# A hybrid attention block on one core: a third of the stick-breaking products on GpSimd, and low parts of the up weight issued after a gate addition

## The chip, the cores and the metric

One Trainium2 chip, one core of it. The metric is the device time of one launch in microseconds, the median of three runs. TensorE is called PE here, VectorE DVE, ScalarE ACT, GpSimd POOL, and SP is the engine whose queue issues nearly all DMAs.

## The reference

One layer over 2048 tokens of width 1024, in float32:

```python
u   = rms_norm(x, norm1_w)
dq, dk, dv, sq, sk, sv = split(u @ w_in)
y_diff = diff_attention(...)           # 4 heads, two softmax maps each
# stick-breaking, 8 heads of 64, strictly causal (s < t):
z = sq @ sk.T * 64 ** -0.5
log_1mb = where(mask, log_sigmoid(-z), 0.0)
rem = cumsum(log_1mb, reverse=True) - log_1mb
a = where(mask, exp(log_sigmoid(z) + rem), 0.0)
y_sb = rms_norm(a @ sv)
h = x + concat(y_diff, y_sb) @ w_out
u2 = rms_norm(h, norm2_w)
out = h + (silu(u2 @ w_gate) * (u2 @ w_up)) @ w_down      # hidden width 2816
```

## The kernel before

Every float32 operand is split into two float16 parts, a high one and a low one, so that a float32 product is three float16 products on PE. The Tile framework orders each engine's instructions: it takes the program's order, priorities and its own estimate of times, and writes one fixed queue per engine. An engine runs its queue in order and waits at each instruction for what it needs.

**Attention, first half of the program.** Eight groups `g` run one after another, four of differential attention (one head each) and four of stick-breaking attention (two heads each). While a group's attention runs, the projection of the next group is fed in between (`proj`, lines 325 to 335); behind the last group the output projection runs (L766). In a stick-breaking group, `stage_a(i, m, b)` handles 128 queries (tile `i`), one head `m` and one block `b` of up to 1024 keys. It goes through the block from the last key to the first in chunks of up to 512 (`c`). Per chunk PE writes the scores into a PSUM bank `sc` (L453), ACT takes sigmoid(-z) into the SBUF tile `om` (L559) and sigmoid(z) in place in the bank (L560), DVE runs a product scan over `om` (L562, which carries from chunk to chunk; its second operand `sc` is bypassed), and DVE multiplies sigmoid(z) with the shifted `om` into the SBUF tile `be` (L563). Tiles `om` and `be` both come from a ring of nine and are called z in the profile. Then `split_t` casts the block's `be` to float16 on ACT (`s`, L89), subtracts on POOL for the low part (L98), and one DMA transposes both (`aT`, L408). `stage_b` multiplies them with the values on PE (`yp`, L463), up to five blocks later (`PD`).

Which engine takes an operation that has a choice is decided by `pick`: it adds the estimated cost to a running load per engine and takes the lowest. `note` adds the loads of operations without a choice, and `level` sets all to zero every four query tiles.

**Feed-forward, second half.** Two token halves of 1024, each in 11 steps of 256 hidden columns (`fg`). A step computes the gate product, then (if two steps have gathered) the down product, and then the up product. In token half 0 the even steps from the third on (i = 2, 4, ..., 10) hold a down product, the odd ones don't. Gate and up are Strassen-Winograd schemes of seven products (`quad`): twelve matmuls of 128 x 512 each (L943), in the order of the code below, into PSUM banks `pa`, `pm` and `pd`. DVE makes the sums: u2 (L956), u3 (L960), c22 (L966, reads `pd`), then L974 and L977. The last product accumulates into the same bank `pd`. In half 0 the weights are prepared on the fly (`load_ffn`): SP loads a float32 buffer `fst`, ACT makes the high parts (L215), POOL forms the Winograd sums (`sx`, and in place in `fst`, L98), and DVE makes the low parts (`split_weight`, L220). A weight has four such pairs: blocks 0-1, 2-3, 4-5 and 6. Blocks 4-5 come out of the in-place sums and are the last in the queues. The up weight of step i is prepared at the end of step i - 1. In half 1 the prepared weights are read back from HBM.

Of the kernel before, what the change touches and what calls it, by code (L numbers as in the profile page):

```python
# [59 lines left out]
def block(tc, a, out):  # L60
# [3 lines left out]
    with top:  # L64
# [8 lines left out]
        def note(e, ns):  # L73
            load[e] += ns * KW[e]
# [34 lines left out]
        def nm(s):  # L109
            uid[0] += 1  # L110
            return f"{s}{uid[0]}"
# [92 lines left out]
            scale_end(lambda m: across(m, pt, cols), rW, pW, junk is not None, sW)  # L204
            return sW

        casts = []

        def behind(k):
            return tc.issue_after(casts[min(k, len(casts) - 1)].ins) if casts else nullcontext()  # L210
# [1 line left out]
        def split_weight(hi, lo, st, n, sW, engines="P"):  # L212
            e = pick(**{k: {"A": 0.84 * n + 200, "D": 0.53 * n + 130, "P": 1.1 * n + 100}[k] for k in engines})
            if e == "A":
                casts.append(ACT.mul(hi, st, sW[:]))  # L215
# [4 lines left out]
            DVE.scalar_tensor_tensor(lo, st, sW[:], hi, op0=ALU.mult, op1=ALU.subtract)  # L220
            note("D", 1.05 * n + 130)

        def norm_tile(xf, xn, wgt, junk=None):
# [32 lines left out]
        with ExitStack() as ph1:  # L256
# [284 lines left out]
            def sb_attn(g, G):  # L541
                last = {}

                @pri("at")
                def stage_a(i, m, b):
                    L = (i + 1) * 128
                    n = min(1024, L - 1024 * b)
                    be, om = z4(), z4()
                    if b == i // 8:
                        DVE.memset(om[:, n : n + 1], 8192.0)  # L550
                    else:
                        DVE.tensor_copy(om[:, n : n + 1], last[m][:, 0:1])
                    last[m] = om
                    for c in range((n - 1) // 512, -1, -1):
                        lo, hi = 512 * c, min(512 * c + 512, n)
                        w = hi - lo
                        sc = ps.tile([P, 512], F32, tag="sc", bufs=4, name=nm("sc"))
                        score_chunk(G, sc, i, 2 * b + c, m, w // P, b == i // 8 and hi == n)
                        ACT.activation(om[:, lo:hi], sc[:, :w], AF.Sigmoid, scale=G["nkz"][:])  # L559
                        ACT.activation(sc[:, :w], sc[:, :w], AF.Sigmoid, scale=G["kz"][:])  # L560
                        ov = om[:, lo:hi][:, ::-1]
                        DVE.tensor_tensor_scan(ov, ov, sc[:, :w], om[:, hi : hi + 1], op0=ALU.mult, op1=ALU.bypass)  # L562
                        DVE.tensor_tensor(be[:, lo:hi], sc[:, :w], om[:, lo + 1 : hi + 1], ALU.mult)  # L563
                        note("A", 1.7 * w + 400)
                        note("D", 3.15 * w + 350)
                    return n, split_t(be[:, :n], n, "A", "P")

                ypd = {}

                def stage_b(i, m, b, n, aT):  # L570
                    r, k = fq(g, i)
                    if i // k not in ypd:
                        ypd[i // k] = ps.tile([P, 512], F32, tag="yp", name=nm("yp"))
                    yp = ypd[i // k]
                    pv(G, yp, P * r + 64 * m, aT, b, n, 128 * m, 64, r == 0 and m == 0 and b == i // 8, r == k - 1 and m == 1 and b == 0)
# [232 lines left out]
        with ExitStack() as ph2:  # L808
# [45 lines left out]
            def load_ffn(half, fg, names, W):  # L854
                eng = "ADP" if fg == 0 else WE
                sc = scales.setdefault(fg, {})
                for nme in names:
# [27 lines left out]
                    sW = sc[nme][2]  # L885
                    tte = "DP" if fg == 0 else "P"
                    casts.clear()
                    sx = fw.tile([P, 512], F32, tag="sx", bufs=1, name=nm("sx"))

                    def put(o, src, n):  # L890
# [52 lines left out]
                        PE.matmul(ps_[:].rearrange("p (t n) -> p t n", n=P), lhsT=wv[:, wo, wi, 128 * kt : 128 * kt + 128], rhs=X[xo][:, :, xi, kt, :], start=start and q == 0, stop=stop and q == 11, skip_group_check=not start)  # L943
                        q += 1

            def quad(wv, X, tag, bufs, c11, hook=None):
                def cst():
                    return fp.tile([P, 512], F32, tag=tag, bufs=bufs, name=nm(tag))

# [16 lines left out]
                DVE.tensor_tensor(c22[:], pd[:], u3[:], ALU.add)  # L966
                c11(1, 1, c22)
                product(pa, wv, 1, X, 1, False, True)
                c11(0, 0, pa)
# [7 lines left out]
                DVE.tensor_tensor(u2[:], u2[:], pd[:], ALU.add)  # L977
                c11(0, 1, u2)

            def gate(W, X, hook=None):  # L980
                sg = {}

                def on_gate(f, t, c):
# [4 lines left out]
                    ACT.activation(s[:], c[:], AF.Silu, scale=W["kg"][:])  # L988
                    sg[f, t] = s

                quad(W["g"], X, "cg", 5, on_gate, hook)
                note("A", 2000)
                return sg

# [126 lines left out]
            W = {}  # L1121
# [35 lines left out]
            for i, (half, fg) in enumerate(steps):  # L1157
# [32 lines left out]
                        tick(3)  # L1190
                    begin("u", *steps[i + 1], "u", Wn) if more else None

                sg = gate(W, X, in_gate)
                if i < 2:
                    tick(3 if i == 0 else 16)
                if not more:
# [38 lines left out]
```

## Time and profile before

| | |
|---|---|
| median of three runs | 2757.65 us (2754.74 to 2759.51) |
| the profiled execution | 2755.86 us, span 2754.1 us |
| stick-breaking groups | about 612 to 1397 us of the span |
| feed-forward, token half 0 | about 1465 to 2140 us |
| DVE products L563 | 320, 193.4 us busy |
| granted PE clock, mean | 0.966 |

In the rows, "out<-in" names tiles without buffer numbers, "x" is a count, and the last part in brackets or behind a bar is the idle time of the engine before the instruction and what ended it. A row of waits gives us in total, times, and the longest. A row in order of time begins with the start and the duration in us. Rows that PE shows as matmuls are pipelined, so a matmul's end overlaps the next one's start.

### The profile page before, as it was taken

The numbers are of one execution on the slowest core, as the hardware profiler recorded it, in microseconds if no ns is written. First come the engines' busy times: TensorE is split into PE (matmuls) and PEld (weight loads), VectorE is DVE, ScalarE is ACT, GpSimd is POOL, SyncE is SP. The second block draws the span as 40 slices with busy tenths as digits, with TensorE's granted clock in tenths as the row PEclk, the third lists the DMA queues.
The fourth block names the chain that finished last, engine by engine and source line by source line (L and its number), as shares of the span: only waits on it lengthen the run. The fifth ranks groups of instructions, "written<-read, shape, count | busy, mean of one in ns | idle before, by whom it ended". The sixth has DMA issues, their size and how long they took to land. (4 is left out here: it accounts for less than half of the span.)

```text
span 2754.1 us, 45485 instructions
## 1 busy us (share of the span) xinstructions
PE 2491.4 (90%) x17084; PEld 1411.9 (51%) x17084; DVE 1997.4 (73%) x3782; ACT 1361.3 (49%) x2543; POOL 1447.6 (53%) x1008
## 2 busy tenths in 40 slices
PE   7998989888888786888989899999999999999998
PEld 4665555555555453457775444444444444444443
DVE  6898879787889989986655877777785544444445
ACT  4665656566878778765644535444352212111121
POOL 2578767655455545546565656565574232322323
PEclk9999999999999987999999999999999999999999
DMA  6788787789999988987797675656658834635534
GB/s 225 201 170 184 148 189 163 173 172 203 196 217 191 198 175 156 199 196 208 199 272 273 218 241 199 220 196 226 235 182 307 315 146 164 229 136 198 207 121 167
DMA packets 649133, 551.91 MB, mean 200 GB/s; under 512 B 506624, under 2 KB 574208, under 8 KB 638672
## 3 DMA queue, kind: packets, MB, share of 16 engines
q1 hardware_dynamic: 647088, 546.92, 72.0%
q8 instruction: 134, 2.20, 0.3%
q0 software_dynamic: 512, 1.36, 0.2%
q10 hardware_dynamic: 1312, 0.72, 0.1%
q14 instruction: 87, 0.71, 0.1%
HBM read 265.27 MB, written 151.52 MB: 151 GB/s over the span
## 5 line engine op out<-in xcount | busy, mean ns | idle before, releaser
L98 POOL TENSOR_TENSOR s<-z,s 128x1024 f16<-128x1024 f32 (+7 forms) x288 | 473.9, 1653 | 334.1 <-ACT s L89 291.2
L325 PE MATMUL pj<-w,xt 128*128 128x384 f16 x3072 | 572.2, 334 | 29.3 <-DVE st L335 12.1
L325 PEld LDWEIGHTS <-xt 128*128 128x128 f16 x3072 | 300.2, 100 | 239.9 <-issue 37.3
L453 PE MATMUL sc<-kT,qT 128*128 128x512 f16 (+3 forms) x1280 | 348.7, 363 | 72.0 <-DVE z L563 33.0
L1041 PE MATMUL pd<-wd,act 128*128 128x512 f16 x1848 | 406.0, 379 | 3.4 <-DVE hs L1047 2.4
L562 DVE TENSOR_TENSOR_SCAN z<-z,sc 128x512 f32<-128x512 f32 (+3 forms) x320 | 355.5, 1113 | 69.4 <-ACT sc L560 67.5
L463 PE MATMUL yp<-v,aT 128*128 128x64 f16 (+1 forms) x4896 | 282.0, 208 | 76.4 <-DMA aT<-s 75.7
L463 PEld LDWEIGHTS <-aT 128*128 128x128 f16 x4896 | 246.5, 102 | 165.1 <-DMA aT<-s 101.7
L943 PEld LDWEIGHTS <-wg 128*128 128x128 f16 x1848 | 182.3, 99 | 247.3 <-issue 37.3
L1041 PEld LDWEIGHTS <-act 128*128 128x128 f16 x1848 | 180.7, 98 | 222.3 <-issue 4.6
L943 PEld LDWEIGHTS <-wu 128*128 128x128 f16 x1848 | 181.8, 98 | 219.7 <-issue 7.2
L98 POOL TENSOR_TENSOR hs<-hs,cu 128x512 f32<-128x512 f32 x132 | 166.8, 1268 | 239.8 <-DVE cu L1047 86.3
L98 POOL TENSOR_TENSOR act<-cg,act 128x512 f16<-128x512 f32 x117 | 166.6, 1437 | 231.4 <-ACT act L999 125.1
L98 POOL TENSOR_TENSOR fst<-fst 128x512 f32<-128x512 f32 x97 | 182.5, 1882 | 157.3 <-DVE wd L220 85.9
L1047 DVE SCALAR_TENSOR_TENSOR hs<-pd,c,hs 128x512 f32<-128x512 f32 x192 | 142.3, 749 | 163.0 <-PE pd L1041 161.5
L89 ACT CAST s<-z 128x384 f16<-128x384 f32 (+7 forms) x216 | 170.2, 789 | 151.5 <-DMA aT<-s 61.9
L559 ACT ACTIVATE z<-sc,c 128x512 f32<-128x512 f32 (+3 forms) x320 | 203.3, 635 | 10.2 <-PE sc L453 6.7
L563 DVE TENSOR_TENSOR z<-sc,z 128x512 f32<-128x512 f32 (+3 forms) x320 | 193.4, 606 | 8.1
L560 ACT ACTIVATE sc<-sc,c 128x512 f32<-128x512 f32 (+3 forms) x320 | 195.6, 611 | 0.0
L999 ACT CAST act<-cg 128x512 f16<-128x512 f32 x132 | 81.3, 616 | 222.1 <-DVE cg L1005 175.8
L766 PE MATMUL po<-wo,mt 128*128 128x256 f16 x1536 | 182.0, 277 | 6.9 <-DVE xf L769 4.9
L943 PE MATMUL pm<-X,wg 128*128 128x512 f16 x792 | 179.1, 379 | 0.2 <-ACT bx L1116 0.2
(233 smaller groups left out, 4026.5 us busy)
## 6 DMA issues: line engine op xcount, KB each, us to landing
xt<-xs SPq DMA_DIRECT2D x112, 512.0 KB, 4.4
hs<-hd SPq DMA_DIRECT2D x96, 512.0 KB, 4.3
hd<-hs SPq DMA_DIRECT2D x80, 512.0 KB, 3.5
split<-wg SPq DMA_DIRECT2D x11, 1792.0 KB, 11.4
split<-wu SPq DMA_DIRECT2D x11, 1792.0 KB, 10.3
split<-wd SPq DMA_DIRECT2D x11, 1792.0 KB, 10.5
wg<-split SPq DMA_DIRECT2D x11, 1792.0 KB, 7.2
wd<-split SPq DMA_DIRECT2D x11, 1792.0 KB, 8.2
```

The costliest lines, as they stand in the source:

```text
L89: ACT.copy(dst, src)
L98: (DVE if e == "D" else POOL).tensor_tensor(dst, a_, b_, op)
L325: PE.matmul(pj[:, :384], lhsT=xv[:, xi, kt, :], rhs=G["w"][:, wi, kt, :], start=n == 0, stop=n == 23)
L453: PE.matmul(sc[:, : 128 * w].rearrange("p (t n) -> p t n", n=P), lhsT=G["q"][i // 4][:, 2 - 2 * o + m, i % 4, :], rhs=G["k"][q][:, m, 0:w, ...
L463: PE.matmul(yp[:, y0 : y0 + wd], lhsT=aT[:, a_, :], rhs=v[:, v_ : v_ + wd], start=start and j == 0 and q == 0, stop=stop and j == nb - 1 a ...
L559: ACT.activation(om[:, lo:hi], sc[:, :w], AF.Sigmoid, scale=G["nkz"][:])
L560: ACT.activation(sc[:, :w], sc[:, :w], AF.Sigmoid, scale=G["kz"][:])
L562: DVE.tensor_tensor_scan(ov, ov, sc[:, :w], om[:, hi : hi + 1], op0=ALU.mult, op1=ALU.bypass)
L563: DVE.tensor_tensor(be[:, lo:hi], sc[:, :w], om[:, lo + 1 : hi + 1], ALU.mult)
L766: PE.matmul(po[:, sl], lhsT=mt[:, kt, P * xi : P * xi + P], rhs=wos[2 * h + n][wi][:, kt, :], start=q == 0, stop=q == 23)
L943: PE.matmul(ps_[:].rearrange("p (t n) -> p t n", n=P), lhsT=wv[:, wo, wi, 128 * kt : 128 * kt + 128], rhs=X[xo][:, :, xi, kt, :], start=st ...
L1041: PE.matmul(po[:], lhsT=act[:, ao, xi, 128 * j : 128 * j + 128], rhs=W["d"][:, wo, wi, :], start=start and u == 0 and q == 0, stop=u == nu ...
```

## The change

**Products.** In `stage_a` a chunk's product gets a choice between DVE and POOL. For a chunk on POOL the second sigmoid writes into `be` in SBUF, since POOL reads no PSUM, and the product is done in place there. The scan stays on DVE and bypasses whatever the bank holds, so there it no longer reads what the second sigmoid writes. The loads that `note` adds for DVE are adapted, which also changes what `pick` gives other operations.

**Low parts.** `split_weight` records its DVE instructions in `lows`. In token half 0, for i > 1, the four low parts of the step's up weight are made to stand in DVE's queue after the addition c22 of the gate product; they wait on nothing more than their place.

```diff
+        def queue_behind(later, first):
+            for z in later:
+                tc.add_manual_dep(z.ins, first.ins.name, mybir.DependencyInfo(mybir.DependencyClass.NoSync, mybir.DependencyReason.DATA), reason="issue order")
...
-            DVE.scalar_tensor_tensor(lo, st, sW[:], hi, op0=ALU.mult, op1=ALU.subtract)
+            lows.append(DVE.scalar_tensor_tensor(lo, st, sW[:], hi, op0=ALU.mult, op1=ALU.subtract))
...
-                        ACT.activation(sc[:, :w], sc[:, :w], AF.Sigmoid, scale=G["kz"][:])
+                        e = pick(D=1.04 * w + 155, P=2.4 * w + 100)
+                        beta = sc[:, :w] if e == "D" else be[:, lo:hi]
+                        ACT.activation(beta, sc[:, :w], AF.Sigmoid, scale=G["kz"][:])
...
-                        DVE.tensor_tensor(be[:, lo:hi], sc[:, :w], om[:, lo + 1 : hi + 1], ALU.mult)
+                        (DVE if e == "D" else POOL).tensor_tensor(be[:, lo:hi], beta, om[:, lo + 1 : hi + 1], ALU.mult)
                         note("A", 1.7 * w + 400)
-                        note("D", 3.15 * w + 350)
+                        note("D", 2.08 * w + 200)
...
                     casts.clear()
+                    lows.clear()
...
-            def quad(wv, X, tag, bufs, c11, hook=None):
+            def quad(wv, X, tag, bufs, c11, hook=None, later=()):
...
-                DVE.tensor_tensor(c22[:], pd[:], u3[:], ALU.add)
+                queue_behind(later, DVE.tensor_tensor(c22[:], pd[:], u3[:], ALU.add))
...
-                sg = gate(W, X, in_gate)
+                sg = gate(W, X, in_gate, list(lows) if half == 0 and i > 1 else ())
```

In the changed kernel's order 148 of the 320 products stand on POOL: 117 of width 512, 6 of 384, 16 of 256 and 9 of 128.

DVE's queue in the second stick-breaking group (i = 14, blocks of two 512-wide chunks; z_12468 and z_12508 are tiles `be`, z_12469 and z_12509 their tiles `om`), before:

```order
L562 SCALAR_TENSOR_TENSOR z_12469<-z_12469,sc_12471 128x512
L563 TENSOR_TENSOR z_12468<-sc_12471,z_12469 128x512
L552 COPY z_12509<-z_12395 128x1
L562 SCALAR_TENSOR_TENSOR z_12469<-z_12469,sc_12478 128x512
L563 TENSOR_TENSOR z_12468<-sc_12478,z_12469 128x512
L562 SCALAR_TENSOR_TENSOR z_12509<-z_12509,sc_12511 128x512
L563 TENSOR_TENSOR z_12508<-sc_12511,z_12509 128x512
```

and in the changed kernel:

```order
L568 SCALAR_TENSOR_TENSOR z_12469<-z_12469,sc_12471 128x512
L569 TENSOR_TENSOR z_12468<-sc_12471,z_12469 128x512
L556 COPY z_12509<-z_12395 128x1
L568 SCALAR_TENSOR_TENSOR z_12469<-z_12469,sc_12478 128x512
L568 SCALAR_TENSOR_TENSOR z_12509<-z_12509,sc_12511 128x512
L569 TENSOR_TENSOR z_12508<-sc_12511,z_12509 128x512
```

The product of the second chunk is gone from DVE, and the next block's scan follows the scan directly.

POOL's queue at the same place in the changed kernel (before, it holds only the rows of L98 there):

```order
L98 TENSOR_TENSOR s_12365<-z_12347,s_12365 128x896
L569 TENSOR_TENSOR z_12468<-z_12468,z_12469 128x512
L98 TENSOR_TENSOR s_12412<-z_12394,s_12412 128x896
L569 TENSOR_TENSOR z_12508<-z_12508,z_12509 128x512
L98 TENSOR_TENSOR s_12485<-z_12468,s_12485 128x1024
```

The moved product of a block stands between the low parts of two earlier blocks, and ahead of its own.

ACT's queue at that place, before:

```order
L560 ACTIVATE sc_12518<-sc_12518,c_8303 128x512
L89 CAST s_12485<-z_12468 128x1024
L559 ACTIVATE z_12586<-sc_12588,c_8304 128x512
L560 ACTIVATE sc_12588<-sc_12588,c_8303 128x512
L559 ACTIVATE z_12586<-sc_12596,c_8304 128x512
```

and in the changed kernel:

```order
L566 ACTIVATE z_12508<-sc_12518,c_8303 128x512
L89 CAST s_12412<-z_12394 128x896
L563 ACTIVATE z_12586<-sc_12588,c_8304 128x512
L566 ACTIVATE sc_12588<-sc_12588,c_8303 128x512
L563 ACTIVATE z_12586<-sc_12596,c_8304 128x512
L566 ACTIVATE z_12585<-sc_12596,c_8303 128x512
L89 CAST s_12485<-z_12468 128x1024
```

The cast of a block (s_12485) now stands two pairs of sigmoids later than it did.

DVE's queue in the feed-forward at an odd step (i = 3; wu_21255 is the step's up weight, cg tiles are the gate sums), before:

```order
L956 TENSOR_TENSOR cg_21298<-pm_21300,cg_21298 128x512
L220 SCALAR_TENSOR_TENSOR wu_21255<-fst_21170,c_21175,wu_21255 128x2x512 x2
L960 TENSOR_TENSOR cg_21327<-pm_21314,cg_21298 128x512
L220 SCALAR_TENSOR_TENSOR wu_21255<-sx_21272,c_21175,wu_21255 128x512
L966 TENSOR_TENSOR cg_21350<-pd_21337,cg_21327 128x512
L220 SCALAR_TENSOR_TENSOR wu_21255<-fst_21170,c_21175,wu_21255 128x2x512
L974 TENSOR_TENSOR cg_21327<-cg_21327,pm_21367 128x512
L977 TENSOR_TENSOR cg_21298<-cg_21298,pd_21337 128x512
```

and in the changed kernel:

```order
L963 TENSOR_TENSOR cg_21298<-pm_21300,cg_21298 128x512
L967 TENSOR_TENSOR cg_21327<-pm_21314,cg_21298 128x512
L973 TENSOR_TENSOR cg_21350<-pd_21337,cg_21327 128x512
L224 SCALAR_TENSOR_TENSOR wu_21255<-fst_21170,c_21175,wu_21255 128x2x512 x2
L224 SCALAR_TENSOR_TENSOR wu_21255<-sx_21272,c_21175,wu_21255 128x512
L981 TENSOR_TENSOR cg_21327<-cg_21327,pm_21367 128x512
L224 SCALAR_TENSOR_TENSOR wu_21255<-fst_21170,c_21175,wu_21255 128x2x512
L984 TENSOR_TENSOR cg_21298<-cg_21298,pd_21337 128x512
```

Three low parts moved from ahead of the third addition (L966, now L973) to behind it; the fourth was behind it already.

More of the change, by code (lines that the diff above doesn't have):

```diff
@@ L205, in weight_scale @@
             return sW
-        casts = []
+        casts, lows = [], []
+        def queue_behind(later, first):
+            for z in later:
+                tc.add_manual_dep(z.ins, first.ins.name, mybir.DependencyInfo(mybir.DependencyClass.NoSync, mybir.DependencyReason.DATA), reason="issue order")
         def behind(k):
@@ L978, in quad, with gate @@
                 c11(0, 1, u2)
-            def gate(W, X, hook=None):
+            def gate(W, X, hook=None, later=()):
                 sg = {}
@@ L989, in on_gate @@
                     sg[f, t] = s
-                quad(W["g"], X, "cg", 5, on_gate, hook)
+                quad(W["g"], X, "cg", 5, on_gate, hook, later)
                 note("A", 2000)
```

## The prediction

> **What bounds the kernel now.** I read the page's totals and slices first, then the busy time by stretch, then the waits of each engine inside the two stretches that the change touches, then the groups for prices, and last the order of time around one addition.
>
> ```profile
> span 2754.1 us, 45485 instructions
> PE 2491.4 (90%) x17084; PEld 1411.9 (51%) x17084; DVE 1997.4 (73%) x3782; ACT 1361.3 (49%) x2543; POOL 1447.6 (53%) x1008
> ...
> DVE  6898879787889989986655877777785544444445
> ```
>
> Averages hide the stages: PE is at 90% over the span, but in the slices of 69 us that hold the stick-breaking heads (the tenth to the eighteenth) VectorE is at 8 or 9 tenths almost throughout, four times at 9. The stretches say it in us:
>
> ```profile
> core 0: us, PE busy (x) PEld busy (x) DVE busy (x) ACT busy (x) POOL busy (x), PEclk, DMA share, GB/s
> 612.00:1200.00 588.00, 473.07 (x4803) 295.59 (x4801) 519.51 (x933) 457.75 (x880) 304.46 (x196) 0.92 0.95 192
> 1050.00:1125.00 75.00, 53.91 (x580) 32.29 (x580) 72.94 (x111) 65.66 (x110) 41.81 (x24) 0.80 0.87 163
> 1200.00:1400.00 200.00, 176.13 (x1826) 145.15 (x1825) 144.86 (x235) 123.42 (x212) 115.22 (x79) 0.96 0.78 198
> 1584.00:2066.00 482.00, 458.61 (x2160) 213.49 (x2160) 373.24 (x530) 211.16 (x251) 302.01 (x194) 0.99 0.62 214
> 1660.00:1703.00 43.00, 39.01 (x190) 18.51 (x188) 38.26 (x55) 26.42 (x31) 30.96 (x20) 1.00 0.59 202
> ```
>
> From 612 to 1200 us VectorE is busy 519.5 of 588 (88%), and in its densest part 72.9 of 75 (97%), while PE falls to 53.9 and its granted clock to 0.80: there VectorE ends last. ScalarE is close behind, 65.7 of 75 (88%). From 1200 to 1400 no engine but PE is near full. From 1584 to 2066 (the first token half of the feed-forward) PE is busy 458.6 of 482, and what it lacks is named by its waits. The waits of PE, VectorE, GpSimd and ScalarE from 612 to 1400, and (last row) of PE from 1570 to 2080:
>
> ```profile
> PE yp L463 <- DMA aT<-s: 49.4, 45, 3.5
> PE sc L453 <- DVE z L563: 33.0, 35, 1.8
> ...
> DVE z L562 <- ACT sc L560: 67.5, 57, 7.1
> ...
> POOL s L98 <- ACT s L89: 287.5, 130, 11.8
> ...
> ACT s L89 <- DMA aT<-s: 42.5, 36, 4.4
> ...
> PE pd L943 <- DVE cg L966: 23.1, 9, 4.4
> ```
>
> In the attention stretch GpSimd mostly waits for ScalarE's cast, so it has room. In the feed-forward nine waits at one line, 23.1 us, are nearly all that PE is not busy from 1584 to 2066 (482 - 458.6 = 23.4): the last gate product adds into the bank that the third addition (L966) has yet to read.
>
> **Part one: products on GpSimd.** Durations, from the groups by shape from 600 to 1400 us and (the first, second and last row) from the page:
>
> ```profile
> L563 DVE TENSOR_TENSOR z<-sc,z 128x512 f32<-128x512 f32 (+3 forms) x320 | 193.4, 606 | 8.1
> L98 POOL TENSOR_TENSOR hs<-hs,cu 128x512 f32<-128x512 f32 x132 | 166.8, 1268 | 239.8 <-DVE cu L1047 86.3
> ...
> L562 DVE TENSOR_TENSOR_SCAN z<-z,sc 128x512 f32<-128x512 f32 x224 | 285.0, 1273 | 41.7 <-ACT sc L560 40.8 <-PE sc L455 0.4
> L559 ACT ACTIVATE z<-sc,c 128x512 f32<-128x512 f32 x224 | 157.0, 701 | 5.9 <-PE sc L453 4.4 <-PE sc L455 1.4
> L563 DVE TENSOR_TENSOR z<-sc,z 128x512 f32<-128x512 f32 x224 | 153.4, 686 | 5.6
> L560 ACT ACTIVATE sc<-sc,c 128x512 f32<-128x512 f32 x224 | 151.8, 678 | 0.0
> L98 POOL TENSOR_TENSOR s<-z,s 128x1024 f16<-128x1024 f32 x84 | 184.7, 2202 | 161.5 <-ACT s L89 147.6 <-issue 9.0 <-DMA aT<-s 3.0
> L89 ACT CAST s<-z 128x1024 f16<-128x1024 f32 x80 | 83.9, 1050 | 70.1 <-DVE z L563 18.7 <-issue 16.1 <-DMA xcd<-x 13.8
> ...
> L98 POOL TENSOR_TENSOR fst<-fst 128x512 f32<-128x512 f32 x97 | 182.5, 1882 | 157.3 <-DVE wd L220 85.9
> ```
>
> The order of the changed kernel holds 148 of the 320 products on GpSimd, 117 of them 512 wide and 31 narrower: nearer half than a third. VectorE loses 117 x 0.686 = 80.3 us, and for the narrow ones 31 x 0.417 ((193.4 - 153.4) / 96) = 12.9: 93 us. GpSimd gains 117 x 1.268 = 148 and, at the same ratio of 1.85, 24: 172 us. No row shows this product on GpSimd; the nearest, two float32 inputs of 512 and no cast, is the 1268 ns one, and 1882 ns (the same shape beside busy VectorE reads) is the upper end. At that end it is 253 us.
>
> Three of the four heads' groups lie before 1200, so there VectorE falls to about 519.5 - 70 = 450 us and GpSimd rises to 304 + 129 = 433. ScalarE, at 458 and unchanged in count, becomes the longest: the second sigmoid still reads PSUM, and writing SBUF costs 701 against 678 ns, 3 us over all 117. For a block of 1024 keys, VectorE now needs 2 x (1.273 + 0.686) = 3.9 us, afterwards with one product moved 3.2; ScalarE needs 2 x (0.701 + 0.678) + 1.05 = 3.8 throughout. So not 93 us are won but what lies between VectorE's and ScalarE's need: in the dense 75 us ScalarE's 65.7 at the 97% that VectorE reaches gives 67.7 (10% less), at 92% it gives 71.4 (5% less). I take 7.5% on the four slices at 9 (275 us: 21 us) and half of that on the four at 8 or just under (275 us: 10 us): 30 us, rounded. Two smaller helps are in it: the scan of a moved chunk no longer waits for the second sigmoid (a share of the 67.5 us), and its score bank comes free without the product (a share of PE's 33.0). After 1200 I put it at nothing: PE's output projections cover VectorE's 28% of free time there. Ends: 0, if ScalarE gets no denser; 70, if ScalarE reaches over the whole 588 us the 88.4% of VectorE (458 / 0.884 = 518). The DMA share of 0.95 there leaves a tenth at most if 1.05 can be held, which I doubt; that is why I stay in the lower half.
>
> The Trainium skill (GPSIMD Engine Reference, section "Performance versus the Vector engine") speaks against this part: for elementwise work with two inputs GpSimd takes 1.96 times as long as VectorE, and it keeps to VectorE for that. The trace agrees on the rate (1268 against 686 ns, 1.85 times). By its advice as a sum, with both engines' time counted, this part would cost 172 - 93 = 79 us instead of giving 30; GpSimd's free time is why I don't follow it.
>
> **Part two: low parts behind the third addition.** VectorE's, PE's, GpSimd's and ScalarE's rows in order of time around an odd step (no down product in it), and VectorE's and PE's around an even one:
>
> ```profile
> 1653.10 0.69 DVE L956 TENSOR_TENSOR cg<-pm,cg 128x512 f32<-128x512 f32 x1
> 1654.66 2.67 DVE L220 SCALAR_TENSOR_TENSOR wu<-fst,c,wu 128x1024 f16<-128x1024 f32 x2 [0.87 <-ACT wu L215]
> 1657.25 0.68 DVE L960 TENSOR_TENSOR cg<-pm,cg 128x512 f32<-128x512 f32 x1
> 1657.86 1.15 DVE L220 SCALAR_TENSOR_TENSOR wu<-sx,c,wu 128x512 f16<-128x512 f32 x1
> 1658.93 0.68 DVE L966 TENSOR_TENSOR cg<-pd,cg 128x512 f32<-128x512 f32 x1
> 1661.35 1.28 DVE L220 SCALAR_TENSOR_TENSOR wu<-fst,c,wu 128x1024 f16<-128x1024 f32 x1 [1.74 <-ACT wu L215]
> ...
> 1650.28 2.75 PE L943 MATMUL pd<-X,wg 128*128 128x512 f16 x12
> 1655.46 2.75 PE L943 MATMUL pm<-X,wg 128*128 128x512 f16 x12
> 1659.66 2.75 PE L943 MATMUL pd<-X,wg 128*128 128x512 f16 x12 [1.45 <-DVE cg L966]
> 1663.12 2.75 PE L943 MATMUL pa<-X,wu 128*128 128x512 f16 x12
> ...
> 1656.28 3.85 POOL L98 TENSOR_TENSOR fst<-fst 128x512 f32<-128x512 f32 x2 [1.22 <-DVE wu L220]
> ...
> 1660.17 1.15 ACT L215 ACTIVATE wu<-fst,c 128x1024 f16<-128x1024 f32 x1 [2.09 <-POOL fst L98]
> ...
> 1695.15 0.68 DVE L956 TENSOR_TENSOR cg<-pm,cg 128x512 f32<-128x512 f32 x1
> 1701.90 0.68 DVE L966 TENSOR_TENSOR cg<-pd,cg 128x512 f32<-128x512 f32 x1
> ...
> 1705.22 16.57 PE L1041 MATMUL pd<-wd,act 128*128 128x512 f16 x76
> 1722.50 18.29 PE L1041 MATMUL pd<-wd,act 128*128 128x512 f16 x84
> ```
>
> The addition's input (the product at 1650.3) is complete at 1653.0, yet it starts at 1658.9, behind three low parts. In the new order L956, L960 and L966 stand together: 1653.1 + 0.69 + 0.68 + 0.68 = 1655.2, which is 3 us before PE, done with the product of 1655.46 at about 1658.2, wants the bank. In the even step the same sum gives 1695.15 + 2.0 = 1697.2 against 1701.9. So the nine waits go: 23.1 us. What now stands behind the addition: the low parts, and behind these the two GpSimd subtractions that overwrite their source, ScalarE's last high part, the last low part. From 1655.2: first two low parts to 1657.9, the subtractions free to start at 1656.7 (1656.28 before), so the last high part moves from 1660.2 to about 1660.6 and the last low part ends near 1663.1. The up weight's first product then starts at 1663.12 - 1.45 = 1661.7, and the second, which reads those blocks, 2.6 us later at 1664.3: 1.2 us to spare. GpSimd's own order is unchanged, and SP's load of the next weight into the same buffer, which waits for the last low part, moves by the same half us. Even steps have the down products between (16.6 + 18.3 us). The last two gate additions come behind low parts, but the order lets one of them pass ahead of the last. Late next is VectorE itself: from 1660 to 1703 it is busy 38.3 us, and PE 39.0, so the stretch cannot shrink far below 39 and a piece of the gain returns there. I take 3 of the 23 back: 20 us. Ends: 23, and 6, if the four odd steps return all of their 4 x 23.1 / 9 = 10.3 us and the five even ones half of 12.8.
>
> **Sum.** The profiled execution took 2755.86 us, 1.8 of it outside the span: 2755.9 - 30 - 20 = 2705.9. The median of the runs shown is 1.8 us above that execution, so 2707.
>
> **Rivals.** (a) The attention stretch keeps its length, since DMA (0.95) and the transposes that PE and ScalarE wait for (49.4 and 42.5 us) or ScalarE's own density set it; part two alone remains: 2756 - 20 = 2736. For it: the DMA share; against it: VectorE at 97% with DMA at 0.87 in the dense part. (b) Part two comes back as a wait for up weights at the four odd steps and a later VectorE: 2756 - 30 + 0 = 2726. (c) ScalarE packs as tightly as VectorE did and PE, no longer starved, gets its clock back (0.92 to near 1): 2756 - 70 - 22 = 2664. (d) Slower: a moved product queues on GpSimd behind a low part of 2.20, then takes 1.27 itself; ScalarE's cast waits behind both, 3.47 us, and the new order covers only two pairs of sigmoids, 2 x (0.701 + 0.678) = 2.76. What is left, 0.71 us, stalls ScalarE, the new longest engine. At 148 products it decides above (50 + 5.5) / (148 x 0.71) = 53% of them finding a low part ahead. With GpSimd 74% busy (433 of 588), 74% do at worst: 78 us, 2756 - 50 + 78 = 2784. Against it: low parts mostly wait now (287.5 us), and with products spread evenly fewer meet one at its start.
>
> **How the numbers follow.** Chances: the forecast 0.55 (its own range 2690 to 2722), (a) 0.18, (b) 0.10, (c) 0.10, (d) 0.07. The range 2672 to 2746 takes in (a), (b) and part of (c), and leaves out (d) and a tail of (c). Within 0.2% (5.5 us, what a measurement of this kernel can tell from no change) falls only (a) with part two near its low end of 6: 0.04. Slower: (d), 0.07. Faster: 0.89.
>
> **What the profile after would show.** Part one: VectorE's products 172 and GpSimd's 148 at 1.2 to 1.4 us, VectorE under 82% and ScalarE over 80% from 612 on, that stretch some 30 us shorter. Part two: the nine waits for the addition gone, no new wait of PE at the up weight's second product. I am wrong if ScalarE's cast waits for GpSimd's products for more than about 30 us, if PE's waits for the transposed tiles grow, or if GpSimd's product takes near 1.9 us.

## The result, and the profile after

The changed kernel takes 2726.53 us (median; 2723.53 to 2731.47) beside 2756.45 for the kernel before: a ratio of 0.9893 with an interval of 0.9878 to 0.9908, about 30 us faster where 50 were forecast. The profiled execution took 2726.11 us. In the changed kernel L943 is L950, L966 is L973, L562 and L563 are L568 and L569, L463 is L467, L220 is L224.

Where the 30 us lie: the first gate product ends attention and opens the feed-forward. From each kernel's answer on the gate line (durations in ns, then first and last start in us), before:

```profile
L943 PE MATMUL pa<-X,wg x528: 376/379/379, 1465.2 to 2663.4; 128*128 128x512 f16 x176
```

and after:

```profile
L950 PE MATMUL pa<-X,wg x528: 376/379/379, 1453.4 to 2633.7; 128*128 128x512 f16 x176
```

The attention half is 11.8 us shorter (1465.2 to 1453.4); from there to the end of the span it is 1288.9 before and 1270.9 after, 18.0 less. These are single executions. A run further down with the same attention program as the change (the products alone) has its first gate product at 1457.4, so such figures are good to some 4 us. The totals and VectorE's slices of the page:

```profile
span 2724.3 us, 45559 instructions
...
PE 2471.4 (91%) x17084; PEld 1404.6 (52%) x17084; DVE 1945.7 (71%) x3716; ACT 1345.8 (49%) x2483; POOL 1569.3 (58%) x1134
...
DVE  6898979698888988876666877777786544444445
```

From the tenth to the eighteenth slice VectorE is at 9 tenths once, where it was four times. VectorE's total fell by 51.7 us (1997.4 to 1945.7), not by the 93 of the moved products: 148 products left it and its count fell by only 66, so 82 other operations came to it on balance, 60 from ScalarE (2543 to 2483) and 22 from GpSimd (1008 + 148 - 1134), as `pick` chose by the changed loads. The same stretches as in the prediction, with the same columns:

```profile
612.00:1200.00 588.00, 480.83 (x4954) 306.77 (x4950) 491.02 (x918) 460.85 (x859) 435.53 (x326) 0.94 1.00 198
1050.00:1125.00 75.00, 54.75 (x626) 34.55 (x625) 63.64 (x108) 63.49 (x113) 57.89 (x40) 0.91 0.90 172
1200.00:1400.00 200.00, 169.49 (x1848) 143.34 (x1847) 134.77 (x193) 113.76 (x187) 124.22 (x84) 0.97 0.78 199
1584.00:2066.00 482.00, 467.91 (x2211) 217.74 (x2210) 372.07 (x536) 210.07 (x250) 304.30 (x195) 0.99 0.63 222
```

VectorE came down from 519.5 to 491.0 of 588 us (the forecast had 450) and in the dense 75 us from 72.9 to 63.6; GpSimd went from 304 to 436, as worked out (433). But ScalarE didn't fill up: 460.9 of 588 (78%), and 63.5 of the dense 75 (85%). No engine is nearly full there now (VectorE, still the longest, is at 84%), while the DMA share went from 0.95 to 1.00.

That share is the time of all packets, added up, over the time of 16 engines, and one is not its upper end: from 700 to 800 us it was 1.06 before and is 1.13 after, since packets overlap. The rows for that stretch, before and after:

```profile
700.00:800.00 100.00, 83.18 (x883) 52.03 (x881) 94.25 (x159) 80.47 (x146) 52.27 (x30) 0.98 1.06 220
```

```profile
700.00:800.00 100.00, 85.47 (x920) 54.32 (x918) 85.28 (x158) 78.07 (x137) 75.53 (x51) 0.98 1.13 215
```

The waits from 612 to 1400 us (in us, times, longest) say what the engines lack:

```profile
POOL s L98 <- ACT s L89: 91.1, 67, 5.0
POOL z L569 <- DVE z L568: 85.6, 61, 6.1
ACT s L89 <- DMA aT<-s: 85.4, 59, 6.0
...
PE yp L467 <- DMA aT<-s: 63.6, 54, 3.7
...
PE sc L457 <- DVE z L568: 16.2, 21, 1.6
DVE xf L775 <- DMA xf<-in_x_dram: 12.0, 3, 4.3
...
ACT s L89 <- POOL z L569: 3.3, 4, 1.2
```

ScalarE's cast waits 85.4 us for a transpose to free a cast tile, where it was 42.5; PE's wait for transposed tiles is 63.6 (49.4 before), which the prediction named as a sign of being wrong. For GpSimd's product itself the cast waits 3.3 us in all. The transposes in turn wait for GpSimd, which makes the low parts: SP's queue, from 612 to 1200 us, before

```profile
SPq L408 <- POOL s L98: 156.0, 88, 6.4
```

and after (L412 is L408):

```profile
SPq L412 <- POOL s L98: 122.5, 68, 5.2
SPq L412 <- POOL z L569: 106.7, 58, 6.4
```

Together 229.2 us where it was 156.0. The groups by shape from 600 to 1400 us give the price of that product, the one unknown:

```profile
L569 POOL TENSOR_TENSOR z<-z,z 128x512 f32<-128x512 f32 x117 | 131.6, 1126 | 89.1 <-DVE z L568 74.0 <-DVE xrs L150 4.4 <-DVE z L554 3.9
L89 ACT CAST s<-z 128x1024 f16<-128x1024 f32 x80 | 84.4, 1057 | 42.2 <-DMA aT<-s 22.8 <-DMA xcd<-x 12.0 <-POOL z L569 3.3
...
L569 DVE TENSOR_TENSOR z<-sc,z 128x512 f32<-128x512 f32 x107 | 73.3, 685 | 3.5
```

In the feed-forward, PE's waits from 1570 to 2080 us:

```profile
PE fsc L177 <- ACT sq L184: 8.5, 3, 3.7
...
PE fsc L886 <- ACT sq L878: 2.2, 2, 1.4
```

The nine waits for the third addition (23.1 us) are gone. In their place PE waits 10.7 us for squares of the next weight (0.3 before). Rows of an odd step in order of time show how:

```profile
1634.99 0.69 DVE L963 TENSOR_TENSOR cg<-pm,cg 128x512 f32<-128x512 f32 x1
1635.78 0.69 DVE L967 TENSOR_TENSOR cg<-pm,cg 128x512 f32<-128x512 f32 x1
1636.61 0.69 DVE L973 TENSOR_TENSOR cg<-pd,cg 128x512 f32<-128x512 f32 x1
1637.21 2.47 DVE L224 SCALAR_TENSOR_TENSOR wu<-fst,c,wu 128x1024 f16<-128x1024 f32 x2
...
1639.92 2.75 PE L950 MATMUL pd<-X,wg 128*128 128x512 f16 x12
...
1643.39 2.75 PE L950 MATMUL pa<-X,wu 128*128 128x512 f16 x12
1643.71 1.29 DVE L224 SCALAR_TENSOR_TENSOR wu<-fst,c,wu 128x1024 f16<-128x1024 f32 x1 [1.75 <-ACT wu L219]
...
1645.02 0.38 SPq L850 DMA_DIRECT2D fst<-in_w_down_dram  x1
...
1645.98 5.34 PE L950 MATMUL pm<-X,wu 128*128 128x512 f16 x24
...
1651.81 1.91 ACT L184 ACTIVATE sq<-fst 128x2048 bf16<-128x2048 f32 x1 [2.06 <-DMA fst<-in_w_down_dram]
...
1653.86 0.30 PEld L177 LDWEIGHTS fsc<-id,m 128*128 128x128 f32 x2 [0.45 <-ACT sq L184]
```

The addition (1636.6) is done well before the last gate product (1639.9), which no longer waits; the last low part ends at 1645.0, before the up weight's second product at 1646.0. But that low part also frees the float32 buffer: the next weight's load is issued at 1645.02, 1.6 us after the up weight's first product. Before, the last low part ended at 1661.35 + 1.28 = 1662.6, half a microsecond ahead of it (1663.12). So the load, the square of what it brings and PE's small product of that square (L177) come some 2 us later in PE's time, and PE waits. Here it waits half a microsecond; in the next odd step the load comes 2.9 us after the up weight's first product, and PE waits 3.75:

```profile
1759.31 2.75 PE L950 MATMUL pa<-X,wu 128*128 128x512 f16 x12
...
1762.24 0.38 SPq L850 DMA_DIRECT2D fst<-in_w_down_dram  x1
...
1770.98 0.80 PE L177 MATMUL fsc<-id,m 128*128 128x128 f32 x2 [3.75 <-ACT sq L184]
```

### The profile page after: what moved, and what is told of

Same layout as the page of the kernel before. It is cut to its first block, busy times and chain, and to the rows that moved or that the text cites. A ratio compares the mean times of both kernels' runs of the same rounds, so it can differ in the third digit from the quotient of the medians.

```text
span 2724.3 us, 45559 instructions
## 1 busy us (share of the span) xinstructions
PE 2471.4 (91%) x17084; PEld 1404.6 (52%) x17084; DVE 1945.7 (71%) x3716; ACT 1345.8 (49%) x2483; POOL 1569.3 (58%) x1134
## 5 line engine op out<-in xcount | busy, mean ns | idle before, releaser
L98 POOL TENSOR_TENSOR s<-z,s 128x1024 f16<-128x1024 f32 (+7 forms) x288 | 477.5, 1667 | 99.3 <-ACT s L89 94.8
L568 DVE TENSOR_TENSOR_SCAN z<-z,sc 128x512 f32<-128x512 f32 (+3 forms) x320 | 352.9, 1112 | 81.4 <-ACT sc L566 39.3
L457 PE MATMUL sc<-kT,qT 128*128 128x512 f16 (+3 forms) x1280 | 339.6, 357 | 51.7 <-DVE z L568 16.2
L467 PE MATMUL yp<-v,aT 128*128 128x64 f16 (+1 forms) x4896 | 279.6, 207 | 91.5 <-DMA aT<-s 90.4
L467 PEld LDWEIGHTS <-aT 128*128 128x128 f16 x4896 | 242.2, 101 | 181.9 <-DMA aT<-s 120.2
L98 POOL TENSOR_TENSOR act<-cg,act 128x512 f16<-128x512 f32 x117 | 166.3, 1434 | 239.4 <-ACT act L1006 133.1
L950 PEld LDWEIGHTS <-wg 128*128 128x128 f16 x1848 | 181.1, 98 | 222.0 <-issue 7.9
L950 PEld LDWEIGHTS <-wu 128*128 128x128 f16 x1848 | 181.9, 99 | 219.0 <-issue 6.5
L98 POOL TENSOR_TENSOR hs<-hs,cu 128x512 f32<-128x512 f32 x132 | 166.9, 1269 | 220.9 <-DVE hs L1054 76.0
L98 POOL TENSOR_TENSOR fst<-fst 128x512 f32<-128x512 f32 x97 | 182.6, 1883 | 161.3 <-DVE wd L224 89.9
L563 ACT ACTIVATE z<-sc,c 128x512 f32<-128x512 f32 (+3 forms) x320 | 207.0, 650 | 25.7 <-PE sc L457 18.5
L569 POOL TENSOR_TENSOR z<-z,z 128x512 f32<-128x512 f32 (+3 forms) x148 | 151.5, 1027 | 100.7 <-DVE z L568 85.6
L950 PE MATMUL pm<-X,wg 128*128 128x512 f16 x792 | 179.7, 380 | 0.0
L950 PE MATMUL pm<-X,wu 128*128 128x512 f16 x792 | 179.4, 379 | 0.0
## 6 DMA issues: line engine op xcount, KB each, us to landing
split<-wu SPq DMA_DIRECT2D x11, 1792.0 KB, 10.4
```

Of the source, the lines that this page charges most:

```text
L98: (DVE if e == "D" else POOL).tensor_tensor(dst, a_, b_, op)
L457: PE.matmul(sc[:, : 128 * w].rearrange("p (t n) -> p t n", n=P), lhsT=G["q"][i // 4][:, 2 - 2 * o + m, i % 4, :], rhs=G["k"][q][:, m, 0:w, ...
L467: PE.matmul(yp[:, y0 : y0 + wd], lhsT=aT[:, a_, :], rhs=v[:, v_ : v_ + wd], start=start and j == 0 and q == 0, stop=stop and j == nb - 1 a ...
L569: (DVE if e == "D" else POOL).tensor_tensor(be[:, lo:hi], beta, om[:, lo + 1 : hi + 1], ALU.mult)
```

## The experiments

The expectations use short names for the theories: A, that the two parts simply add; T, that products moved in the last group give time back at its end; S, that ScalarE caps attention; M, that the transposes cap it; P, that PE's projections do; R1 and R2, that a lack of cast tiles is new with the change or was there before it. The other letters are explained where they stand. Ratios are to the kernel before, timed beside each run, with their 95% interval.

**Each part alone.** The products without the moved low parts:

```diff
-                sg = gate(W, X, in_gate, list(lows) if half == 0 and i > 1 else ())
+                sg = gate(W, X, in_gate)
```

> The changed kernel without the second part: products are shared with GpSimd, the low parts of the up weight stand where they stood before. The profile of the changed kernel has the first gate product 11.7 us earlier (1465.0 to 1453.3) and the rest of the span 18.1 us shorter. Theory A (the two parts act in different halves of the program and add): 12 us faster than before (2744 to 2747), with the nine waits of PE for the third gate addition back at about 23 us. Theory B (part of the later saving comes from the attention half running ahead): 20 us or more faster.

Measured: 2742.32 us, ratio 0.9935 (0.9923 to 0.9946). PE's first wait from 1570 to 2080 us is again the old one:

```profile
PE pd L950 <- DVE cg L973: 22.4, 9, 4.5
```

The low parts without the products:

```diff
-                        e = pick(D=1.04 * w + 155, P=2.4 * w + 100)
+                        e = pick(D=1.04 * w + 155)
```

> Low parts behind the third addition, all products on VectorE as before. Theory A (parts add): 18 us faster than before (2737 to 2741), the nine waits gone. Theory B: 10 us faster or less.

Measured: 2742.08 us, ratio 0.9944 (0.9926 to 0.9961). The new waits for squares come with the low parts alone:

```profile
PE fsc L177 <- ACT sq L184: 7.9, 3, 3.4
...
PE fsc L886 <- ACT sq L878: 2.5, 2, 1.3
```

The parts add: 0.9935 x 0.9944 = 0.9879, within the interval of the whole change (0.9878 to 0.9908). Of 2757 us the products give 18 (15 to 21), the low parts 15 (11 to 20); theory A had taken 12 and 18 from the profiles. So the larger part of the miss lies in part one.

**The last group.** No products on GpSimd in the last group, whose end the output projection follows:

```diff
-                        e = pick(D=1.04 * w + 155, P=2.4 * w + 100)
+                        e = pick(D=1.04 * w + 155, **({"P": 2.4 * w + 100} if g < NG - 1 else {}))
```

> The changed kernel with GpSimd allowed for products only in the first three stick-breaking groups; in the last one all stay on VectorE. The changed kernel reached its 264th scan near 1171 us where before it was 1200, but kept only 11.7 us of these 28 at the first gate product. Theory T (the last group gives it back by its own moved products and by the output projection's operations that the loads push to other engines): 6 to 15 us faster than the changed kernel (2712 to 2720). Rival P (PE sets the length from there on, with matmuls left over from the earlier groups: 2530 matmuls after that point against 2411): the same as the changed kernel within 4 us. Rival D (the moved products help in every group alike): 3 us or more slower than the changed kernel.

Measured: 2720.97 us, ratio 0.9861 (0.9844 to 0.9879); the span of its profile is 2720.7, 3.6 less than after. By the ratios that is 9 us faster than the change, (0.9893 - 0.9861) x 2757, as T has it, but the intervals touch, and the first gate product is only 1.5 us earlier (1451.9). The 28 us that T started from aren't in the rows either: the 264th scan starts at 1168.4 us where before it was 1186.4, 18 earlier. So leaving the products of the last group on VectorE loses nothing; that moving them costs something isn't settled.

**ScalarE or the transposes.** If ScalarE's load set the pace, giving VectorE, which now has room, some of the casts would help:

```diff
-                    return n, split_t(be[:, :n], n, "A", "P")
+                    return n, split_t(be[:, :n], n, "AD", "P")
```

> The changed kernel, in which the cast of a stick-breaking block to its high part may go to VectorE too (some 40 of them go there), so that ScalarE, which I took for the next longest engine, is relieved by about 40 us. Theory S (ScalarE's time sets the stretch now): 5 us or more faster than the changed kernel (below 2721). Rival D (transposes and the ring of cast tiles set it; ScalarE waits 85.4 us for cast tiles still being transposed): the same within 4 us, ScalarE's share lower and its wait for transposed tiles longer.

Measured: 2745.4 us, ratio 0.9945 (0.9931 to 0.9959): 14 us slower than the change, (0.9945 - 0.9893) x 2757. ScalarE's load fell to 440.1 of 588 us, and it didn't help. The waits from 612 to 1400 us:

```profile
ACT s L89 <- DMA aT<-s: 71.1, 46, 4.5
...
DVE s L91 <- DMA aT<-s: 19.4, 17, 3.2
```

The wait for a cast tile went along with the cast: VectorE now stands 19.4 us for transposes, in a queue that also holds the scans. Less work on ScalarE didn't shorten the stretch, which speaks against S, but the edit brought that new wait along, and neither theory had 14 us slower.

For M the transposes were halved, in the kernel before and in the one with the products: only the high part is transposed, and the third product of scores and values reads the high part once more, so the number of matmuls stays.

```diff
-                SP.dma_start_transpose(aT[:, : 2 * n // P, :], s16[:, : 2 * n])
+                SP.dma_start_transpose(aT[:, : n // P, :], s16[:, :n])
...
-                    for q, (a_, v_) in enumerate(((j, o), (j, o + wd), (nb + j, o))):
+                    for q, (a_, v_) in enumerate(((j, o), (j, o + wd), (j, o))):
```

> The kernel before, with only the high half of each attention block transposed by DMA (the low half is left out, and the third product reads the high half again): half the transpose traffic, same matmuls. Base for the next kernel. Theory M (transposes cap the stretch): clearly faster than before, 15 us or more. Theory L (VectorE ends last there): within 8 us of before.

> The same half transposes with the products shared with GpSimd and the low parts left in place. Against the half-transpose base: theory M (DMA transposes and the ring behind them took the other half of the forecast 30 us): 27 us or more faster than that base, where the products alone gave 17 us. Theory P (PE's projections took it): 14 to 20 us faster than that base, as without it.

Measured: 2709.82 us without the products (ratio 0.9818, 0.98 to 0.9836) and 2672.73 with them (0.9688, 0.9673 to 0.9703). The products give 37 us here, 2709.82 - 2672.73, against 18 with full transposes (the first gate product goes from 1422.5 to 1389.4, by 33). The stretch from 612 to 1200 us, without the products:

```profile
612.00:1200.00 588.00, 483.43 (x4992) 304.08 (x4990) 540.43 (x972) 469.30 (x913) 311.64 (x205) 0.94 0.69 149
```

and with them:

```profile
612.00:1200.00 588.00, 505.44 (x5338) 329.46 (x5337) 516.84 (x945) 474.61 (x880) 453.80 (x343) 0.95 0.71 157
```

Without the products VectorE reaches 540.4 of 588 (92%): with the transposes out of the way it is the bound that the prediction took it for. With them PE does 7% more matmuls in the same time. So something in the way over the transposes capped what the products could give. It need not be their bytes: a transpose of the high part alone no longer waits for the low part that GpSimd makes (SP's waits for GpSimd's low part are 1.7 us without the products, 156.0 in the kernel before), so fewer bytes and an earlier start are not told apart by this pair.

**The projections.** If PE's share of projections capped attention, a shorter projection would bring the products' gain out. The third of its three products is left out, in the kernel before and in the one with the products (and the low parts in their old place):

```diff
-                    for xi, wi in ((0, 0), (0, 1), (1, 0)):
-                        PE.matmul(pj[:, :384], lhsT=xv[:, xi, kt, :], rhs=G["w"][:, wi, kt, :], start=n == 0, stop=n == 23)
+                    for xi, wi in ((0, 0), (0, 1)):
+                        PE.matmul(pj[:, :384], lhsT=xv[:, xi, kt, :], rhs=G["w"][:, wi, kt, :], start=n == 0, stop=n == 15)
```

> The kernel before, with the projection's third product (low part of the activations times high part of the weight) left out: 16 instead of 24 matmuls a tile in all eight groups. Base for the next kernel; faster than before by the differential groups, where PE is at 91%, by 40 us or more; in the stick-breaking groups by little if VectorE ends last there.

> The short projection with the products shared with GpSimd. Against the short-projection base: theory P (at the ends of the groups PE has the next group's projection left over and takes back what the dense middle won): 25 us or more faster than that base. Theory M (DMA): 14 to 20 us, as without it.

Measured: 2710.75 us without the products (0.9826, 0.9811 to 0.9841) and 2716.53 with them (0.9844, 0.9828 to 0.9859): the products give nothing. P falls. That the products' 18 us would vanish too was not expected. The stretch from 612 to 1200 us, without the products:

```profile
612.00:1200.00 588.00, 432.61 (x4472) 269.48 (x4471) 531.08 (x935) 463.81 (x882) 303.52 (x196) 0.85 0.95 191
```

and with them:

```profile
612.00:1200.00 588.00, 430.81 (x4445) 269.66 (x4443) 476.59 (x862) 451.46 (x833) 425.92 (x321) 0.84 0.94 189
```

VectorE fell by 54 us and nothing moved faster; DMA stands at 0.94 to 0.95 and ScalarE's wait for transposes rose from 28.1 to 63.8 us. That fits M in its direction, but M had 14 to 20 us of gain, the granted clock also fell to 0.85, and the cause was not tested further.

**The order of the low parts.** To free the buffer sooner, the first of the four low parts may stand ahead of the addition again:

```diff
-                sg = gate(W, X, in_gate, list(lows) if half == 0 and i > 1 else ())
+                sg = gate(W, X, in_gate, lows[1:] if half == 0 and i > 1 else ())
```

> The changed kernel, but the first of the four low parts stays ahead of the third addition; only the last three are put behind it. GpSimd's in-place sums wait for that first one alone, and the weight buffer, the next weight's load and ScalarE's square follow them. Theory W (the whole move made the buffer free later and gave some 8 to 13 us back as PE's waits for squares, L177 and L886): 4 to 9 us faster than the changed kernel (0.986 to 0.988 of before), these waits of PE under 5 us from 1540 to 2120, the wait for the addition still near 0. Rival V (VectorE is simply the longest in those steps): the same as the changed kernel within 3 us.

Measured: 2725.56 us, ratio 0.9863 (0.9842 to 0.9883). PE's waits from 1570 to 2080 us:

```profile
PE fsc L177 <- ACT sq L184: 4.6, 2, 2.4
PE fsc L886 <- ACT sq L878: 3.4, 2, 1.8
...
PE pd L950 <- DVE cg L973: 1.7, 1, 1.7
```

The squares' waits fall from 10.7 to 8.0 us, not under 5 as theory W had it, and 1.7 us of the addition's come back; the stretch from the first gate product to the end is 3 us shorter (1267.7). The two waits trade against each other, as the buffer's story says. The ratio lies in W's range, but its interval overlaps that of the change, so the time doesn't decide.

**A fourth cast tile.** ScalarE's wait says that no cast tile is free, so the ring of three was made four, once at the cost of a transposed tile, once of a tile z, and once (of a tile z) in the kernel before:

```diff
-QB, KB, ZB, AB, SB, PD = 4, 7, 9, 5, 3, 5
+QB, KB, ZB, AB, SB, PD = 4, 7, 9, 4, 4, 5
```

> The changed kernel with a ring of four cast tiles s in place of three, and four transposed tiles aT in place of five (the memory has no room for both). Theory R (the ring of three holds ScalarE up while tiles wait to be transposed): ScalarE's wait for transposes falls from 85 to under 50 us and the kernel is 6 us or more faster than the changed one (below 0.987 of before). Theory B (the transposes' traffic itself is the cap): within 4 us of the changed kernel, the wait moves elsewhere.

Measured: 2724.43 us, ratio 0.9865 (0.9838 to 0.9893), in theory R's range but not to be told from the change; ScalarE's wait for transposes is 41.5 us.

```diff
-QB, KB, ZB, AB, SB, PD = 4, 7, 9, 5, 3, 5
+QB, KB, ZB, AB, SB, PD = 4, 7, 8, 5, 4, 5
```

> The changed kernel with four cast tiles s and eight tiles z in place of nine. Theory R: as for the other ring, 6 us or more faster than the changed kernel, unless the eight z tiles cost it. Theory B (traffic): within 4 us or slower.

> The kernel before, with four cast tiles s in place of three and eight z tiles in place of nine, the same rings that made the changed kernel 20 us faster. Theory R1 (before the change VectorE was late enough that the ring of three hardly held anyone; the ring took its price only once products had moved): within 6 us of before (0.998 to 1.002). Rival R2 (the ring cost the kernel before as much, it is a gain of its own): 14 us or more faster than before (below 0.995).

Measured: 2713.17 us with the change (0.9822, 0.9796 to 0.9847), the fastest complete version of this study, and 2732.78 without it (0.9901, 0.9884 to 0.9917). The rings were short before the change already (R2): four cast tiles with eight tiles z are worth 27 us there and about 20 with the change, (0.9893 - 0.9822) x 2757. What one tile z less does by itself was not run. With the change, ScalarE's wait from 612 to 1400 us:

```profile
ACT s L89 <- DMA aT<-s: 28.0, 21, 5.9
```

and the scans' and the gate's lines (durations, then first and last start):

```profile
L568 DVE TENSOR_TENSOR_SCAN z<-z,sc x320: 453/1270/1282, 612.6 to 1363.9; 128x512 f32<-128x512 f32 x88, 128x128 f32<-128x128 f32 x24, 128x256 f32<-128x256 f32 x24, 128x384 f32<-128x384 f32 x24
```

```profile
L950 PE MATMUL pm<-X,wg x792: 379/379/379, 1439.0 to 2621.8; 128*128 128x512 f16 x198
...
L950 PE MATMUL pa<-X,wg x528: 376/379/379, 1443.4 to 2619.2; 128*128 128x512 f16 x176
```

In the kernel before with the same ring, the wait:

```profile
ACT s L89 <- DMA aT<-s: 7.0, 8, 1.9
```

and the scans' and the gate's lines:

```profile
L562 DVE TENSOR_TENSOR_SCAN z<-z,sc x320: 453/1270/1281, 610.7 to 1374.1; 128x512 f32<-128x512 f32 x88, 128x128 f32<-128x128 f32 x24, 128x256 f32<-128x256 f32 x24, 128x384 f32<-128x384 f32 x24
```

```profile
L943 PE MATMUL pa<-X,wg x528: 376/379/379, 1443.5 to 2640.8; 128*128 128x512 f16 x176
```

The two kernels open the gate with different products: with the change PE begins with the bank `pm` at 1439.0, without it with `pa` at 1443.5, so the `pa` lines alone mislead. So with four cast tiles the whole change starts the gate 4.5 us earlier, where with three it was 11.8, and its last scan starts 10.2 us earlier (1374.1 to 1363.9), where it was 15.9 (1395.6 to 1379.7). From the first gate product to the end it is 2709.9 - 1439.0 = 1270.9 beside 2731.4 - 1443.5 = 1287.9, 17.0 us less, close to the 18.0 of the main pair. By the ratios the whole change is worth 22 us here, (0.9901 - 0.9822) x 2757. With the scatter of some 4 us, the products give little at the gate here; that they give nothing isn't shown. From 612 to 1200 us the share of DMA is 1.00 with the change and 0.96 without.

## Why the prediction was right and wrong

The sign and the range held, and both parts gave time, each less than forecast; 20 of the 50 us didn't come.

**Part two: 15 for 20, right in size, partly wrong in how.** The addition starts 3 us before PE wants the bank, the nine waits went, and the up weight's second product doesn't wait, as worked out. Three of 23 us were to come back as VectorE's own density. What came back were 10.7 - 0.3 = 10.4 us of waits for squares, which leaves 23.1 - 10.4 = 12.7 of the waits, in line with the 15 (11 to 20). The step that failed is the clause on SP's load of the next weight, "moves by the same half us": half a microsecond was measured against VectorE's old times, but PE had moved forward by the wait that went, so against PE the load is 2 us later or more. It was left out that a release which keeps its time comes late for an engine that has moved forward.

**Part one: 18 for 30, the term that was mis-sized.** VectorE did stop being nearly full. The step that failed is "ScalarE, at 458 and unchanged in count, becomes the longest", with the 450 us for VectorE ahead of it; the waits for transposes were left to rival (a). VectorE came to 491, since of the 93 us only 52 left it on balance, and 60 operations of ScalarE's were among those that came to it. ScalarE stayed at 78%, not over 80, and its cast tiles were what it waited for. Two of the prediction's own signs failed with it: VectorE under 82% (84 from 612 to 1200 us), and no growth of PE's waits for transposed tiles (63.6 us after 49.4). Rival (a) had a chance of 0.18 and was set aside by one row: VectorE at 97% with DMA at 0.87 in 75 us. That row holds where it stands, but over the 588 us VectorE was at 88%. The half-transpose pair has the same operations moved between engines, and there the products give 37 us, more than the 30 that were meant. So it is the way over the transposes that kept them from it. The four-tile pair points the same way, with 4.5 us of the change left at the gate, but from one execution each.

What it is in that way was not separated: the packets, SP's issue, or the wait for GpSimd's low part. In the kernel before, packets of 256 bytes are the transposes' (their count falls from 263,936 to 151,680 between 612 and 1200 us when the transposes are halved). They took 24.2 ns each, 263,936 x 24.2 / 16 = 399 us per DMA engine in 588 us; after, 267,280 x 25.0 / 16 = 418. Since packets overlap, this doesn't say that the engines are full, and after the change no packet is under way in 7% of the 588 us (10% before). SP's queue is held 2.1 us (mean) by a transpose, after the change 169 of them 358 of 588 us, and it waits for GpSimd as shown above, 229.2 us where it was 156.0.

That wait points to a second piece that works against the products. In order, each cast of ScalarE's was matched with its low part and its transpose: from the end of a cast to the start of its low part it was 0.27 us before (mean of 161 between 612 and 1200 us) and 0.99 after (167), since the low part now stands behind a product in GpSimd's queue. From a cast's start to the end of its transpose's issue it rose from 5.76 to 6.60. As an estimate, with three cast tiles that is 0.84 / 3 = 0.28 us per cast, over 167 casts 47 us; ScalarE's wait grew by 40 in these 588 us (35.7 to 75.6). That the two are near each other doesn't show the cause. Rival (d) had GpSimd's queue, but made the cast wait for the product; by these rows the queue acts one step on, through the cast tile. With a fourth tile that wait falls to 28.0, but the gate starts only 4.5 us ahead of the kernel before with the same ring, so this piece doesn't account for all that is missing.

**After 1200 us: "nothing" was about 4 us short.** From the issue of attention's last store to the first gate product it is 46.3 us before (1418.9 to 1465.2) and 50.8 after (1402.6 to 1453.4). VectorE's additions of the output waited 12.0 us for the input x, 1.8 before. The kernel without moved products in the last group has 46.5 (1405.4 to 1451.9) and 3.1 us of that wait. Two more runs with the change's attention have 50.4 and 50.9 with 12.3 and 11.9 us of wait, but the one with casts on VectorE has 53.0 with a wait of 0.8. So the 4 us go with the moved products, and the wait for x isn't shown to be their cause.

**The price of the product** was 1126 ns, below the 1268 that the nearest row gave and far from the upper end of 1882; it did not decide. The Trainium skill (GPSIMD Engine Reference, section "Performance versus the Vector engine") gives 4497 ns for an addition of two float32 tiles of 2048; a quarter is 1124, an estimate that the trace bears out. Its advice to keep elementwise work on VectorE holds for the single operation (1126 against 685 ns), but not for this stage: added up over both engines the part would have cost 79 us, and it gained 18.

## What to carry to other kernels

When work is taken off the busiest engine, the gain ends at the next limit of that stage. Look for it in what the next engine waits for (here ScalarE and PE, for transposes) over the whole stage, whatever the densest 75 us say. When an automatic choice fills engines by estimated load, count what it moves onto the engine that was relieved: here 41 of 93 us came back. Where a wait of PE goes, measure every buffer's release against PE's new time and not against its own old one. Before moving work to relieve an engine that waits for tiles, try one tile more in that ring: here four cast tiles, with eight tiles z for nine, gave the kernel before 27 us.

## What was not expected of the hardware

- The product of two float32 tiles of 512 on GpSimd, written in place, took 1126 ns, faster than the two-input operation of the same shape that the prediction took its price from (1268).
- DMA's share went to 1.00 over 588 us, and to 1.13 in 100 of them, without a longer landing: the median from issue to landing of a transpose stayed at 4.4 us (3.2 when halved). In the kernel before, transposes moved 263,936 x 256 bytes / 588 us = 115 GB/s over the stage, and 225 in their densest 5 us (244 after). The Trainium skill (DMA: Bandwidth & Descriptors, section "Latency and other measured facts") gives 261 GB/s for a strided DMA transpose; only such short stretches came near it.
- Halving the transposes, and with it the wait for the low part, took 51 us off the kernel before, more than the whole change.
- With shorter projections the granted clock fell to 0.85 from 612 to 1200 us (0.92 before), as PE's share of busy time fell from 80% to 74% (473.1 to 432.6 of 588). In the kernel before, the stretches shown have the same order: 0.80 at 72% (53.9 of 75), 0.99 at 95% (458.6 of 482). The cause was not tested.
